# Low-rank maps and decay sums of an RWKV-7 mixer: from fp32 products to split float32r products

## The chip, the cores and the metric

The kernel runs on one core of a Trainium2 chip. The metric is the device time of one execution in microseconds (us). A core has TensorE (PE; its weight loads, PEld, run beside the products), VectorE (DVE), ScalarE (ACT), GpSimd (POOL) and SyncE (SP), whose queue issues most DMA transfers. Each engine works through its own instructions in order; semaphores make one engine wait for another.

## The reference, cut to what matters

One decoder layer over 512 tokens of width 1024: RMSNorm, one input projection that feeds two mixers (differential attention and RWKV-7 time mixing), an output projection, a layer of retrieved experts over 16384 experts, and a gated embedding. What matters here is how the time mixing gets its decay and its gate `a`:

```
w = -softplus(-(w0 + tanh(xw) @ w_up)) - 0.5      # 64 -> 512
a = sigmoid(a0 + xa @ a_up)                       # 64 -> 512
decay = exp(-exp(w))
state = state * decay + sa kk*a + v k             # token after token
```

Since exp(w) = exp(-0.5) * sigmoid(w0 + tanh(xw) @ w_up), the log of a product of decays is -exp(-0.5) times a sum of sigmoids. The kernel works in chunks of 32 tokens and needs, for each token, the sum over its chunk up to it (inclusive and exclusive) and from it to the chunk's end.

## The kernel before, in words

The 512 tokens are four blocks b of 128 (a token to a partition). The mixer stage (`mixers`) first projects the time mixing's keys, low-rank inputs, receptances and values, then walks the four blocks with `rw_prepare`, and after that solves a triangular system (`rw_solve`), builds the states (`rw_states`), and forms the outputs (`rw_out`), with the attention (`da_block`) among them. `out_proj`, the expert stage (`retrieve`, `peer`) and the tail follow.

Most products of the kernel are made from split operands: `split` has ScalarE copy x into a float32r tile hi (L129) and VectorE or GpSimd subtract, lo = x - hi (L133, L135), and three products hi·hi, hi·lo, lo·hi add up in PSUM (L201 to L203 for the input projections). The products of `rw_prepare` are plain fp32.

For a block, `rw_prepare` transposes the low-rank inputs (ptl, L466 to L468), copies two of them to SBUF (lw, L471, with a row of ones from a memset, L470, for the bias), and makes plw = lw0 · w_up (L475) and pla = lw1 · a_up (L479), each 65 rows deep and 512 columns wide. ScalarE turns them into sw and aa by a sigmoid (L477, L481). pcum = tri_le · sw (L484) and prem = tri_gt · sw (L491) are the sums over the chunk; the matrices hold -exp(-0.5) where they are not zero. ppc (L495) gives the sums of whole chunks. VectorE adds exp(-0.5) sw to pcum (e_ex, L486), and ScalarE takes the exponentials e_in, e_inv, e_ex, e_end and pcc (L487 to L497). A run of VectorE products then makes al, rt, be, kt, bh and kh, TensorE transposes four of them (ptr, L531) and makes the masked products psA (L549). Before that `rw_keys` norms the keys kk on VectorE, with a chain of 128x8 operations (L90 to L99).

The source weaves the attention's projections among the blocks as filler for TensorE (`WEAVE`: one step of eight k-chunks per yield), and in blocks 2 and 3 steps of the first solve (`PACE`). The order on each engine is laid down when the program is built, by a scheduler that starts from the source's order, takes the instructions that its estimates call ready, and gives out pages and buffers as it goes; so an instruction may stand earlier on its engine than in the source, and a tile may have to wait for the last reader of the page it got.

Memory: `p2` gives pages of 128x512 fp32 from a pool of 28, `p4` pages of 128x1024 from a pool of 14; nearly all tiles of the mixer are such pages. `small` tiles have two buffers each. PSUM accumulators `acc` have four. Constants (`mixer_consts`) are made on GpSimd at the start of the kernel; w_up and a_up, 65x512 each with the bias as last row, are loaded by four DMAs on SP's queue.

Of the kernel before, what the change touches and what calls it, by code (L numbers as in the profile page):

```python
# [8 lines left out]
F32 = mybir.dt.float32  # L9
F32R = mybir.dt.float32r  # L10
# [3 lines left out]
AF = mybir.ActivationFunctionType  # L14
OP = mybir.AluOpType
# [13 lines left out]
EXPH = math.exp(-0.5)  # L29
# [25 lines left out]
class Kernel:  # L55
# [188 lines left out]
    def mixer_consts(self, pool):  # L244
        nc, a = self.nc, self.a
# [17 lines left out]

        self.tri_le = pool.tile([128, 128], F32, name="tri_le")
        nc.gpsimd.memset(self.tri_le, -EXPH)
        same_chunk(self.tri_le, 0)
        self.tri_gt = pool.tile([128, 128], F32, name="tri_gt")
        nc.gpsimd.memset(self.tri_gt, -EXPH)
        same_chunk(self.tri_gt, 2)
        self.mask2 = pool.tile([128, 2, 128], F32, name="mask2")  # L270
# [9 lines left out]

        causal = pool.tile([128, 128], F32, name="causal")
        nc.gpsimd.memset(causal, 0.0)
# [6 lines left out]

        self.w_up = pool.tile([65, 512], F32, name="w_up")  # L290
        nc.sync.dma_start(self.w_up[0:64, :], a["rw_w_up"])
        nc.sync.dma_start(self.w_up[64:65, :], a["rw_w0"])
        self.a_up = pool.tile([65, 512], F32, name="a_up")
        nc.sync.dma_start(self.a_up[0:64, :], a["rw_a_up"])
        nc.sync.dma_start(self.a_up[64:65, :], a["rw_a0"])
        self.k_k = self.load_bcast(pool, "rw_k_k", 512)
# [106 lines left out]
    def p2(self, name, shape=(128, 512), dt=F32):  # L403
        return self.pages.tile(list(shape), dt, name=name, tag="p2", bufs=28)

# [50 lines left out]
    def rw_prepare(self, b, psum, r, k, v, kk, lx, st):  # L456

        nc = self.nc
        ident, sm, p2, p4 = self.ident, self.small, self.p2, self.p4
# [5 lines left out]
        pt = psum.tile([128, 3, 128], F32, name="ptl", tag="tp")  # L465
        nc.tensor.transpose(pt[0:64, 0, :], lx[:, 0:64], ident)  # L466
        nc.tensor.transpose(pt[0:64, 1, :], lx[:, 64:128], ident)
        nc.tensor.transpose(pt[:, 2, :], lx[:, 128:256], ident)  # L468
        lw = sm.tile([65, 2, 128], F32, name="lw")
        nc.vector.memset(lw[64:65, :, :], 1.0)  # L470
        nc.vector.tensor_copy(lw[0:64, :, :], pt[0:64, 0:2, :])  # L471
        st["lg"] = sm.tile([128, 128], F32, name="lg", bufs=NB)
        nc.vector.tensor_copy(st["lg"], pt[:, 2, :])
        p1 = psum.tile([128, 512], F32, name="plw", tag="mm")
        nc.tensor.matmul(p1, lw[:, 0, :], self.w_up, start=True, stop=True)  # L475
        sw = p2("sw")
        nc.scalar.activation(sw, p1, AF.Sigmoid)  # L477
        pa = psum.tile([128, 512], F32, name="pla", tag="mm")
        nc.tensor.matmul(pa, lw[:, 1, :], self.a_up, start=True, stop=True)  # L479
        aa = p2("aa")  # L480
        nc.scalar.activation(aa, pa, AF.Sigmoid)  # L481

        pc = psum.tile([128, 512], F32, name="pcum", tag="mm")
        nc.tensor.matmul(pc, self.tri_le, sw, start=True, stop=True)  # L484
        e_in, e_inv, e_ex, e_end = p2("e_in"), p2("e_inv"), p2("e_ex"), p2("e_end")
        nc.vector.scalar_tensor_tensor(e_ex, sw, EXPH, pc, op0=OP.mult, op1=OP.add)  # L486
        nc.scalar.activation(e_in, pc, AF.Exp)  # L487
        nc.scalar.activation(e_inv, pc, AF.Exp, scale=-1.0)
        nc.scalar.activation(e_ex, e_ex, AF.Exp)
        pr = psum.tile([128, 512], F32, name="prem", tag="mm")  # L490
        nc.tensor.matmul(pr, self.tri_gt, sw, start=True, stop=True)  # L491
        nc.scalar.activation(e_end, pr, AF.Exp)
        pp = psum.tile([128, 4, 4], F32, name="ppc", tag="tp")
# [34 lines left out]
        for src, dst in ((be, bet), (al, art[:, :, 0, :]), (rt, art[:, :, 1, :]), (kt, ktt)):  # L528
            pt = psum.tile([128, 4, 128], F32, name="ptr", tag="tp")
# [1080 lines left out]
```

## Time and profile before

| | |
|---|---|
| median of 3 runs | 1838.44 us (1831.96 to 1841.31) |
| the profiled execution | 1837.09 us, span 1835.4 us |
| granted TensorE clock, mean | 0.969 of 2.4 GHz |
| busy | PE 94%, PEld 80%, DVE 78%, ACT 41%, POOL 33% of the span |
| the four blocks of `rw_prepare` | from 104 us (first lw) to about 274 us (last akv) |

The profile is one execution; a time in it is counted from the start of its span. Busy shares are means over stages with different limits. "Granted clock" is the share of TensorE's full clock that it got; it has two levels, 0.5 (1.2 GHz) and 1.0 (2.4 GHz), and a mean between them is a mix in time.

### The profile page before, as it was taken

What the parts mean: (1) busy time and instruction counts of PE and PEld (TensorE: products, weight loads), DVE (VectorE), ACT (ScalarE), POOL (GpSimd) and SP (SyncE); (2) the same over time, 40 slices, a digit from 0 to 9 for tenths busy, and PEclk for the clock granted to TensorE, in tenths of its full rate; (3) what the DMA queues carried; (4) which work ended last, traced back from release to release, by engine and by line L of the source; (5) the groups of instructions that cost most, each with busy time, mean ns of one, the idle gap of its engine ahead of it and who ended that gap; (6) DMA issues with size and microseconds to landing.
All of it is one profiled execution on the core that took longest, in us unless ns stands there. A gap on an engine that the chain in (4) does not pass through costs nothing.

```text
span 1835.4 us, 28662 instructions
## 1 busy us (share of the span) xinstructions
PE 1728.9 (94%) x10458; PEld 1468.2 (80%) x10458; DVE 1425.6 (78%) x3216; ACT 746.7 (41%) x1382; POOL 604.7 (33%) x425
## 2 busy tenths in 40 slices
PE   7889996998899888999999999999999999999998
PEld 6766764766777787998777888889899999999986
DVE  5366787675569998888888888887888888888885
ACT  5353332432345654444344333333333333333354
POOL 2650011111046663001111133234545555555530
PEclk9896996999999999999999999999999999999999
DMA  7451233433332343446666587778989898989891
GB/s 232 137 149 55 75 114 79 129 80 127 117 120 71 125 127 115 132 139 216 206 209 197 187 272 249 254 246 292 313 302 317 300 316 303 312 303 316 303 332 58
DMA packets 150417, 363.71 MB, mean 198 GB/s; under 512 B 43922, under 2 KB 58510, under 8 KB 150148
## 3 DMA queue, kind: packets, MB, share of 16 engines
q1 hardware_dynamic: 113412, 227.65, 38.7%
q0 software_dynamic: 36864, 134.23, 21.5%
q8 instruction: 82, 1.34, 0.3%
q14 instruction: 59, 0.48, 0.1%
HBM read 332.61 MB, written 21.36 MB: 193 GB/s over the span
## 4 chain that ended last, share of the span: by engine, by line
PE 67%; DVE 19%; issue 3%; ACT 3%; POOL 0%; DMA 0%; SPq 0%; DVEq 0%; ACTq 0%; POOLq 0%
PE po L1278 21%; PE phid L1142 8%; PE phid L1144 8%; PE phid L1143 8%; PE pg L1247 2%; DVE wlo L133 2%; PE psA L549 2%; DVE ids L1091 2%; ACT whi L129 1%; DVE rest L985 1%; PE psS L765 1%; DVE jj L1235 1%; PE accr L239 1%; PE accr L237 1%; PE accr L238 1%
## 5 line engine op out<-in xcount | busy, mean ns | idle before, releaser
L133 DVE TENSOR_TENSOR wlo<-wraw,whi 128x1024 fp32r<-128x1024 f32 x243 | 297.5, 1224 | 150.6 <-ACT whi L129 150.5
L129 ACT ACTIVATE whi<-wraw 128x1024 fp32r<-128x1024 f32 x276 | 291.4, 1057 | 171.3 <-PE phid L1143 59.0
L1144 PE MATMUL phid<-u2dhi,wlo 128*128 128x384 f32 x1024 | 347.3, 339 | 12.8 <-POOL wlo L133 12.8
L1142 PE MATMUL phid<-u2dhi,whi 128*128 128x384 f32 x1024 | 350.4, 342 | 1.0 <-ACT row L1151 1.0
L1143 PE MATMUL phid<-u2dlo,whi 128*128 128x384 f32 x1024 | 346.4, 338 | 0.0
L1301 POOL DMA_INDIRECT row<-in_peer_u_dram,idx x128 | 189.8, 1483 | 403.2 <-DVE row L1313 219.7
L1301 POOL DMA_INDIRECT row<-in_peer_v_dram,idx x128 | 186.1, 1454 | 277.0 <-DVE h L1317 194.7
L1278 PE MATMUL po<-whi,chi 128*128 128x512 f32 x768 | 243.9, 398 | 1.2 <-ACT row L1151 1.2
L1278 PE MATMUL po<-whi,clo 128*128 128x512 f32 x768 | 243.1, 398 | 1.7 <-DVE clo L135 0.4
L1278 PE MATMUL po<-wlo,chi 128*128 128x512 f32 x768 | 241.4, 395 | 0.0
L1144 PEld LDWEIGHTS phid<-u2dhi,wlo 128*128 128x128 f32 x1024 | 194.3, 190 | 14.8 <-POOL wlo L133 14.7
L1142 PEld LDWEIGHTS phid<-u2dhi,whi 128*128 128x128 f32 x1024 | 194.6, 190 | 5.8 <-ACT row L1151 1.3
L1143 PEld LDWEIGHTS phid<-u2dlo,whi 128*128 128x128 f32 x1024 | 194.1, 190 | 3.7
L1278 PEld LDWEIGHTS po<-whi,clo 128*128 128x128 f32 x768 | 143.0, 188 | 42.3 <-DVE clo L135 9.0
L1278 PEld LDWEIGHTS po<-wlo,chi 128*128 128x128 f32 x768 | 144.4, 188 | 34.2
L1317 DVE SCALAR_TENSOR_TENSOR h<-row,ids,h 128x1024 f32<-128x1024 f32 x128 | 164.0, 1281 | 1.6
L129 ACT ACTIVATE chi<-gelu 128x384 fp32r<-128x384 f32 x128 | 67.4, 526 | 240.1 <-DVE gelu L1255 121.8
L1278 PEld LDWEIGHTS po<-whi,chi 128*128 128x128 f32 x768 | 141.1, 188 | 25.6 <-ACT row L1151 1.5
L1313 DVE SCALAR_TENSOR_TENSOR row<-row,xn 128x1024 f32<-128x1024 f32 x128 | 153.7, 1220 | 0.0
L1151 ACT ACTIVATE gelu<-phid 128x384 f32<-128x384 f32 x86 | 42.3, 492 | 266.9 <-PE phid L1144 266.9
L133 POOL TENSOR_TENSOR wlo<-wraw,whi 128x1024 fp32r<-128x1024 f32 x33 | 78.4, 2386 | 126.4 <-ACT whi L129 114.7
L201 PE MATMUL acc<-whi,uhi 128*128 128x512 f32 (+1 forms) x224 | 89.6, 404 | 16.7 <-ACT whi L129 9.5
(439 smaller groups left out, 2884.7 us busy)
## 6 DMA issues: line engine op xcount, KB each, us to landing
wraw<-in_peer_uT_dram SPq DMA_DIRECT2D x128, 512.0 KB
wraw<-in_peer_v_dram SPq DMA_DIRECT2D x128, 512.0 KB
wraw<-in_w_in_dram SPq DMA_DIRECT2D x24, 512.0 KB
wraw<-in_peer_w_q_dram SPq DMA_DIRECT2D x16, 512.0 KB
ahead<-row SPq DMA_DIRECT2D x42, 192.0 KB
gelu<-ahead SPq DMA_DIRECT2D x42, 192.0 KB
wraw<-in_w_out_dram SPq DMA_DIRECT2D x8, 512.0 KB
zp<-z SPq DMA_DIRECT2D x12, 224.0 KB
```

What stands on the lines that cost most here:

```text
L129: self.last_hi = nc.scalar.activation(hi, src, AF.Copy, **({} if g is None else {"scale": g}))
L133: self.last_lo = eng.tensor_tensor(lo, src, hi.bitcast(F32), op=OP.subtract)
L201: nc.tensor.matmul(o, hi[:, k, s], whi, start=(k == 0), stop=False)
L549: nc.tensor.matmul(ps[:, mm, :, :], lhs[q, m * 128:(m + 1) * 128], art[q, m, :, :], start=True, stop=True)
L1142: nc.tensor.matmul(ps, whi[:, s], hi[:, k, :], start=(k == 0), stop=False)
L1143: nc.tensor.matmul(ps, whi[:, s], lo[:, k, :], start=False, stop=False)
L1144: nc.tensor.matmul(ps, wlo[:, s], hi[:, k, :], start=False, stop=(k == KC - 1))
L1151: nc.scalar.activation(g, ps, AF.Gelu)
L1278: nc.tensor.matmul(outs[b, e], lhs[:, s], rhs[:, 512 * e:512 * e + 512], start=(c == 0 and rhs is vhi and lhs is chi), stop=(c == NKEY - 1 ...
L1301: nc.gpsimd.indirect_dma_start(out=row, out_offset=None, in_=a["peer_u" if kind == "U" else "peer_v"], in_offset=bass.IndirectOffsetOnAxis ...
L1313: nc.vector.scalar_tensor_tensor(row, row, 1.0, xn0, op0=OP.mult, op1=OP.mult, accum_out=hid0[:, k:k + 1])
L1317: nc.vector.scalar_tensor_tensor(acc0, row, hid0[:, k:k + 1], acc0, op0=OP.mult, op1=OP.add)
```

## The change

The four fp32 products per block become float32r products of split operands. w_up and a_up are split once, on GpSimd, into hi and lo; lw is split per block (hi by VectorE's copy, lo by a VectorE subtraction; row of ones: 1 in hi, 0 in lo), and plw and pla take three products each. sw is split by the helper `split` (hi by ScalarE, lo by VectorE); the triangular matrices hold 1 in place of -exp(-0.5), which float32r holds exactly, so pcum and prem take two products each. The factor -exp(-0.5) goes into the scale of the exponentials, and e_ex becomes pcum - sw. ppc is left as it is. lw's two tiles have one buffer each, where lw had two. `p2` has 26 pages where it had 28; masks are drawn up in p2 pages, and raw weights are loaded into them.

```diff
-        self.tri_le = pool.tile([128, 128], F32, name="tri_le")
-        nc.gpsimd.memset(self.tri_le, -EXPH)
-        same_chunk(self.tri_le, 0)
-        self.tri_gt = pool.tile([128, 128], F32, name="tri_gt")
-        nc.gpsimd.memset(self.tri_gt, -EXPH)
-        same_chunk(self.tri_gt, 2)
+        tri = []
+        for i in (0, 2):
+            x = self.p2("tri", [128, 128])
+            nc.gpsimd.memset(x, 1.0)
+            same_chunk(x, i)
+            tri.append(pool.tile([128, 128], F32R, name=f"tri{i}"))
+            nc.gpsimd.tensor_copy(tri[-1], x)
+        self.tri_le, self.tri_gt = tri
...
-        causal = pool.tile([128, 128], F32, name="causal")
+        causal = self.p2("causal", [128, 128])
...
-        self.w_up = pool.tile([65, 512], F32, name="w_up")
-        nc.sync.dma_start(self.w_up[0:64, :], a["rw_w_up"])
-        nc.sync.dma_start(self.w_up[64:65, :], a["rw_w0"])
-        self.a_up = pool.tile([65, 512], F32, name="a_up")
-        nc.sync.dma_start(self.a_up[0:64, :], a["rw_a_up"])
-        nc.sync.dma_start(self.a_up[64:65, :], a["rw_a0"])
+        self.w_up, self.a_up = [], []
+        for x, up, bias in ((self.w_up, "rw_w_up", "rw_w0"), (self.a_up, "rw_a_up", "rw_a0")):
+            raw = self.p2("up")
+            nc.sync.dma_start(raw[0:64, :], a[up])
+            nc.sync.dma_start(raw[64:65, :], a[bias])
+            x += [pool.tile([65, 512], F32R, name=f"{up}{y}") for y in ("hi", "lo")]
+            nc.gpsimd.tensor_copy(x[0], raw[0:65, :])
+            nc.gpsimd.tensor_tensor(x[1], raw[0:65, :], x[0].bitcast(F32), op=OP.subtract)
...
-        return self.pages.tile(list(shape), dt, name=name, tag="p2", bufs=28)
+        return self.pages.tile(list(shape), dt, name=name, tag="p2", bufs=26)
...
-        lw = sm.tile([65, 2, 128], F32, name="lw")
-        nc.vector.memset(lw[64:65, :, :], 1.0)
-        nc.vector.tensor_copy(lw[0:64, :, :], pt[0:64, 0:2, :])
+        lw = [sm.tile([65, 2, 128], F32R, name=f"lw{x}", bufs=1) for x in ("hi", "lo")]
+        for x, one in zip(lw, (1.0, 0.0)):
+            nc.vector.memset(x[64:65, :, :].bitcast(F32), one)
+        nc.vector.tensor_copy(lw[0][0:64, :, :], pt[0:64, 0:2, :])
+        nc.vector.tensor_tensor(lw[1][0:64, :, :], pt[0:64, 0:2, :], lw[0][0:64, :, :].bitcast(F32), op=OP.subtract)
...
-        p1 = psum.tile([128, 512], F32, name="plw", tag="mm")
-        nc.tensor.matmul(p1, lw[:, 0, :], self.w_up, start=True, stop=True)
+        def up(i, w, name):
+            ps = psum.tile([128, 512], F32, name=name, tag="mm")
+            nc.tensor.matmul(ps, lw[0][:, i, :], w[0], start=True, stop=False)
+            nc.tensor.matmul(ps, lw[0][:, i, :], w[1], start=False, stop=False)
+            nc.tensor.matmul(ps, lw[1][:, i, :], w[0], start=False, stop=True)
+            return ps
+        p1 = up(0, self.w_up, "plw")
         sw = p2("sw")
         nc.scalar.activation(sw, p1, AF.Sigmoid)
-        pa = psum.tile([128, 512], F32, name="pla", tag="mm")
-        nc.tensor.matmul(pa, lw[:, 1, :], self.a_up, start=True, stop=True)
+        swh, swl = (p2(x, dt=F32R) for x in ("swhi", "swlo"))
+        self.split(swh, swl, sw)
+        pa = up(1, self.a_up, "pla")
         aa = p2("aa")
         nc.scalar.activation(aa, pa, AF.Sigmoid)
         pc = psum.tile([128, 512], F32, name="pcum", tag="mm")
-        nc.tensor.matmul(pc, self.tri_le, sw, start=True, stop=True)
+        for x, y in ((swh, True), (swl, False)):
+            nc.tensor.matmul(pc, self.tri_le, x, start=y, stop=not y)
...
-        nc.vector.scalar_tensor_tensor(e_ex, sw, EXPH, pc, op0=OP.mult, op1=OP.add)
-        nc.scalar.activation(e_in, pc, AF.Exp)
-        nc.scalar.activation(e_inv, pc, AF.Exp, scale=-1.0)
-        nc.scalar.activation(e_ex, e_ex, AF.Exp)
+        nc.vector.tensor_tensor(e_ex, pc, sw, op=OP.subtract)
+        nc.scalar.activation(e_in, pc, AF.Exp, scale=-EXPH)
+        nc.scalar.activation(e_inv, pc, AF.Exp, scale=EXPH)
+        nc.scalar.activation(e_ex, e_ex, AF.Exp, scale=-EXPH)
         pr = psum.tile([128, 512], F32, name="prem", tag="mm")
-        nc.tensor.matmul(pr, self.tri_gt, sw, start=True, stop=True)
-        nc.scalar.activation(e_end, pr, AF.Exp)
+        for x, y in ((swh, True), (swl, False)):
+            nc.tensor.matmul(pr, self.tri_gt, x, start=y, stop=not y)
+        nc.scalar.activation(e_end, pr, AF.Exp, scale=-EXPH)
```

## Rows read from the trace of the kernel before

**Rows 1.** The page: busy time by engine, and the last chain by line.

```profile
PE 1728.9 (94%) x10458; PEld 1468.2 (80%) x10458; DVE 1425.6 (78%) x3216; ACT 746.7 (41%) x1382; POOL 604.7 (33%) x425
...
PE po L1278 21%; PE phid L1142 8%; PE phid L1144 8%; PE phid L1143 8%; PE pg L1247 2%; DVE wlo L133 2%; PE psA L549 2%; DVE ids L1091 2%; ACT whi L129 1%; DVE rest L985 1%; PE psS L765 1%; DVE jj L1235 1%; PE accr L239 1%; PE accr L237 1%; PE accr L238 1%
```

**Rows 2.** Windows: length, busy us (and instructions) by engine, granted clock, DMA.

```profile
128.00:170.00 42.00, 32.13 (x113) 22.02 (x112) 27.41 (x69) 16.52 (x28) 2.28 (x2) 0.63 0.25 78
...
196.00:262.00 66.00, 62.07 (x288) 44.62 (x288) 60.15 (x175) 31.65 (x55) 2.04 (x5) 0.95 0.27 79
```

**Rows 3.** Chain of waits in order of time (start, us, what), block 2.

```profile
199.65 0.23 PE acc L201
199.88 0.86 PE pcum L484 x2
```

**Rows 4.** The same chain after block 1 and in block 3.

```profile
172.57 0.43 PE acc L202
...
241.68 1.71 PE pcum L484 x2
```

**Rows 5.** Groups by line: ScalarE's split copy (min/median/max ns), VectorE's subtraction and copy (mean).

```profile
L129 ACT ACTIVATE u2hi<-tps x8: 577/597/598, 488.5 to 496.3; 128x512 fp32r<-128x512 f32 x8
...
L133 DVE TENSOR_TENSOR u2lo<-tps,u2hi 128x512 fp32r<-128x512 f32 x8 | 5.4, 690 | 2.1 <-ACT u2hi L129 2.0
...
L471 DVE COPY lw<-ptl 64x256 f32<-64x256 f32 x4 | 1.6, 410 | 6.0 <-PE ptl L468 6.0
```

**Rows 6.** Timeline of all engines in block 0; in brackets the idle time before.

```profile
127.91 1.12 DVE L90 TENSOR_SCALAR knxh<-knr 128x8 f32<-128x8 f32 x1
...
129.08 1.27 POOL L437 TENSOR_TENSOR zs<-z,zp 128x512 f32<-128x512 f32 x1
...
130.42 0.17 DVE L97 TENSOR_TENSOR knxi<-knx,knxh 128x8 f32<-128x8 f32 x1
...
133.04 0.68 DVE L486 SCALAR_TENSOR_TENSOR e_ex<-sw,pcum 128x512 f32<-128x512 f32 x1
...
138.14 0.69 DVE L510 TENSOR_TENSOR be<-aa,e_inv 128x512 f32<-128x512 f32 x1
...
138.98 1.08 PE L531 MATMUL ptr<-ident,be 128*128 128x128 f32 x4 [7.09 <-DVE be L510]
```

**Rows 7.** Chain of waits in order of time, block 1.

```profile
162.67 1.72 PE pla L479 x2
...
164.49 0.27 DVE lw L470
...
167.03 0.61 DVE e_ex L486
...
169.82 0.59 ACT z L879
```

**Rows 8.** Timeline of all engines in block 2.

```profile
207.30 0.68 DVE L510 TENSOR_TENSOR be<-aa,e_inv 128x512 f32<-128x512 f32 x1
...
210.26 0.60 PE L531 MATMUL ptr<-ident,be 128*128 128x128 f32 x4
```

**Rows 9.** Waits from 225 to 262 us: who waited for whom, total, times, longest.

```profile
DVE e_ex L486 <- PE pcum L484: 0.9, 1, 0.9
```

**Rows 10.** Tile zp: GpSimd's first operation on it after the set-up.

```profile
L434 POOL TENSOR_TENSOR zp<-zp,z x16: 743/1286/1748, 38.8 to 126.1; 128x512 f32<-128x512 f32 x12, 128x256 f32<-128x256 f32 x4
```

**Rows 11.** Windows as in rows 2, around block 0's end and in block 1.

```profile
134.00:136.00 2.00, 0.00 (x0) 0.00 (x0) 2.00 (x4) 1.89 (x4) 0.00 (x0) 0.60 0.32 103
...
144.00:146.00 2.00, 1.30 (x6) 0.47 (x5) 1.19 (x4) 0.00 (x0) 0.00 (x0) 0.84 0.27 87
...
148.00:150.00 2.00, 2.00 (x8) 1.48 (x7) 0.74 (x3) 0.00 (x0) 0.00 (x0) 0.52 0.37 78
```

**Rows 12.** Waits from 270 to 480 us, as in rows 9.

```profile
POOL bv L692 <- DMA pd<-pp: 15.4, 1, 15.4
...
ACT pexp L770 <- issue: 12.3, 1, 12.3
```

## The prediction

> **What bounds the kernel now.** I read the page first. TensorE is busy for most of the span, and most of the chain that ended last lies on it [rows 1]; but the lines that carry that chain are those of the expert stage (L1142 to L1144, L1278), and the change touches none of them. It touches the mixer: sixteen products (four in each of four token blocks of rw_prepare), their preparation, and the pool of pages they live in. So its worth is read from the stretch of those four blocks, 104 to 262 us, and the page's shares say nothing of it. The windows show two regimes there [rows 2]. From 128 to 170 us TensorE is busy 32.13 of 42 us at a mean granted clock of 0.63: nothing fills its gaps, and what counts is the latency through ScalarE and VectorE. From 196 to 262 us TensorE (62.07 of 66) and VectorE (60.15 of 66) are both nearly full. Only in the second regime can saved TensorE time become saved time, and there added VectorE time costs nearly as much. What the mixer saves or loses passes on to the end: out_proj and the expert stage begin when it is done.
>
> **The change, priced.** A fp32 product of 512 columns runs as two instructions and takes 0.86 us at 2.4 GHz, a float32r product 0.23 [rows 3]. At 1.2 GHz they take 1.71 and 0.43 us [rows 4]. A block loses four fp32 products and gains ten float32r ones (3+3+2+2): 3.44 - 2.33 = 1.11 us saved at the high level, 6.84 - 4.3 = 2.54 at the low one. Blocks 0 and 2 are at the high level, 1 and 3 mostly at the low one: 7.3 us of TensorE time in all.
>
> Added per block: one ScalarE copy of 128x512 into fp32r (the nearest row, from PSUM: 0.597 us), one VectorE subtraction of 128x512 (nearest row 690 ns; back to back such operations start 0.60 apart), a subtraction of 64x256 (the copy of that shape takes 0.41) [rows 5] and one more memset (0.27) [rows 7]. The e_ex operation keeps its engine, shape and class; the factor inside the exponentials is a scale that e_inv has already: both nothing. ScalarE is idle around each addition, except that aa now starts one copy (0.5 to 0.6 us) after sw; aa is not needed before ka, so I cost that at nothing; without that cover it is 0.6 a block.
>
> What matters is the new wait. Before, pcum needed sw alone. Now its second half needs sw, then the ScalarE copy, then a VectorE subtraction that queues in order behind the thirteen small operations of the key norm (L90 to L99, L451). Behind the waiting pcum stand prem, ppc and all later TensorE work; e_ex and the exponentials wait for it. Block by block:
>
> Block 0. TensorE stands idle 7.09 us until be is there (138.14) [rows 6], so its saving is worth nothing. VectorE runs without a gap from the key norm through e_ex (133.04) to be. The subtraction adds 0.6 to that run, and if it stands after kk, pcum's second half and its hand-over come between (0.4 to 0.6 more), partly filled by the two wlo operations behind e_ex. Bounds +0.6 and +1.8; I take +0.9, nearest the VectorE row.
>
> In block 0 the rows also show VectorE's 128x8 operation L90 taking 1.12 us while GpSimd works on zp and zs, where one of that size right after them takes 0.17; GpSimd's last such operation runs 129.08 to 130.35 [rows 6]. By the Trainium skill (SBUF — State Buffer, section "Who interferes with whom") a VectorE instruction with two SBUF inputs and a GpSimd instruction that reads SBUF exclude each other for the whole instruction; the new subtraction has two such inputs. The trace agrees that one can hold the other. By that rule the subtraction could start up to 1.27 us late here and the sum below would be +1.7 in place of +0.4; by the rows alone it stands in the queue behind the key norm, whose first operations are held already, and pays nothing more. I go by the row.
>
> Block 1. The chain runs pla, a memset of lw for a later block that waits for pla at the head of VectorE's queue, the key norm, e_ex, the exponentials, the eviction z, TensorE again [rows 7]. plw and pla shrink by 0.42 each (1.71 - 3 x 0.43), so the memset gets free 0.84 earlier; there are two of them now (+0.2), and the subtraction adds 0.6, perhaps with pcum's second half (0.43 and the hand-over) behind it. ScalarE's sw stays where its table load puts it. Bounds -0.3 and +0.7; I take +0.2. The rest of the saving is idle time before z.
>
> Block 2. Here TensorE is on the chain with projections as filler: -1.11 at best. Against it: lo and hi of lw have one buffer each instead of two, so the memsets for block 3 now wait for block 2's pla, about 0.8 us, at the head of VectorE's queue, and the subtraction comes after: e_ex up to 1.8 us later. That is nearly covered: be was ready at 207.98 and TensorE turned to it at 210.26 [rows 8], 2.3 us of slack. Bounds -1.1 and +0.7; I take -0.4.
>
> Block 3. At the low level from plw on [rows 4]: plw, pla and pcum shrink, less the stall for the subtraction, which queues among the solver's VectorE steps: about -1.2 on TensorE. VectorE gets 1.0 more but loses a wait of 0.9 for pcum [rows 9]. The two meet again at ptr (258 us), near level: bounds -1.2 and +1.0; I take -0.3.
>
> Set-up. GpSimd makes masks and casts them, and now splits w_up and a_up (two casts, two subtractions of 65x512; nearest row 1.27 for 128x512 [rows 6]). The loads are the same four on SP's queue, the results are not wanted before block 0, and the next work in GpSimd's queue, zp, begins at 38.8 us [rows 10]. So nothing; the upper bound is 2.6, were VectorE held for both subtractions while TensorE waits for it.
>
> Sum: +0.9 + 0.2 - 0.4 - 0.3 = **+0.4 us**, against the profiled execution's 1837.09 (span 1835.4, 1.7 around it). The median of the runs shown, 1838.44, lies 1.35 above that. 0.4 on it gives **1838.8**, said as 1839. With all lower bounds (-2.0) 1836.4; with all upper ones, set-up and port included (+8.1), 1846.5.
>
> **Rivals.** (A) TensorE is the bound in all four blocks and the whole 7.3 us is kept: 1831.1. For it: its share of the windows from 196 us on. Against it: the 7.09 us wait in block 0 and the chain through VectorE in block 1. Chance 0.13.
>
> (B) The clock. It falls in 134 to 136 us (mean 0.60), after TensorE had stood idle since 132, and again at 148 (0.52 in 148 to 150) after TensorE was busy only 1.30 us of 144 to 146 [rows 11]. From there to the end of pla at 164.39 TensorE works at 1.2 GHz and is nearly all of the chain: 16.4 us of it would be 8.2 at 2.4 GHz. The change puts prem and ppc later, into the hole before 138.98, and shifts every later phase by some tenths; the second fall need not come. With block 3 kept whole (2.54) this gives 1838.44 - 10.7 = 1827.7. Against it: the work that precedes the fall is untouched. The same lottery can lose in block 2, which ran at 1.00. Chance 0.17.
>
> (C) Slower: pages. The p2 pool goes from 28 pages to 26, and each block holds two more for a while (swhi, swlo). By the code, v, qT, rtT and dav hold 16 pages until the end of the mixer, and in the mixer's last part two solver pages, up to five states, y, ysq, rwg, bv, the loads bhr and ykr and the pp pages come on top: about 28. The trace shows page waits there: bv waited 15.4 us for the store of pp, and an exponential waited 12.3 us on ScalarE with no releaser shown [rows 12], which I read as a wait for a page of p4. bv's wait cost nothing. If two pages fewer put such a wait on SP's queue (bhr and ykr, with the loads of the next block behind them) or on a state, the mixer's rw chain stops for about that long: 1838.8 + 12.3 = 1851. It decides as soon as the waiting page is not bv's. Against it: by my count the four blocks themselves need about 25. Chance 0.18.
>
> **The numbers.** Forecast 0.52, A 0.13, B 0.17, C 0.18. A measurement of this kernel can tell about 0.5%, 9.2 us, from no change: faster means under 1829.2, slower over 1847.6. B and the best of A (0.03) are faster: 0.20. C is slower: 0.18. The rest is the same: 0.62. The forecast's own range is 1836 to 1847; taking in A, most of B and C leaves 1826 to 1851, with under 2 in 10 outside.
>
> **What would show it.** Right: pcum's second product in each block waits for the subtraction, TensorE's wait for be in block 0 is no shorter, be comes 0.5 to 2 us later there, memsets of lw hold VectorE in blocks 1 and 2, and the mixer ends within 3 us of before. Wrong: 196 to 262 us gets shorter by over 3 us (A); the clock is 1.00 in 148 to 164 (B); states, SP loads or evictions after 282 us wait with no work of their own outstanding (C).

## The result, and the profile after

The changed kernel takes **1853.34 us** (median of 18 runs, 1842.18 to 1863.07), the kernel before 1841.76 in 18 runs of the same session: a ratio of **1.0066, interval 1.0044 to 1.0087**, some 12 us slower. The forecast was 1839, no change, and the median lies above the range's end of 1851. The profiled execution has a span of 1847.2 us and a mean granted clock of 0.961 (before 1835.4 and 0.969).

The page of the changed kernel: busy time by engine and the last chain by line, as [rows 1].

```profile
PE 1738.3 (94%) x10466; PEld 1475.7 (80%) x10466; DVE 1429.3 (77%) x3228; ACT 759.8 (41%) x1394; POOL 609.1 (33%) x431
...
PE po L1295 21%; PE phid L1159 8%; PE phid L1161 8%; PE phid L1160 8%; PE pg L1264 2%; DVE wlo L133 2%; PE acc L202 2%; ACT whi L129 2%; PE acc L203 2%; PE acc L201 2%; DVE ids L1108 1%; PE psA L566 1%; PE psS L782 1%; DVE rest L1002 1%; DVE jj L1252 1%
```

TensorE was to lose 7.3 us of work and is 9.4 us longer busy: less work, but at a lower clock. ScalarE grew by 13.1 us where four copies of 0.6 us were expected. The windows that answer to [rows 2]:

```profile
128.00:170.00 42.00, 25.15 (x113) 18.00 (x113) 31.07 (x75) 22.27 (x33) 1.15 (x1) 0.70 0.21 64
...
196.00:262.00 66.00, 59.41 (x268) 44.35 (x268) 58.09 (x170) 34.16 (x55) 0.86 (x4) 0.87 0.22 65
```

In the first stretch TensorE is busy 7.0 us less and ScalarE 5.8 us more than before; the second is 2.7 us less busy on TensorE, with 20 products fewer in it and at a clock of 0.87 in place of 0.95. ScalarE's growth is in its table loads. The groups by line, kernel after (30 loads in all):

```profile
L491 ACT ACT_TABLE_LOAD x4 | 5.1, 1283 | 0.1
L514 ACT ACT_TABLE_LOAD x4 | 5.1, 1283 | 0.1
L496 ACT ACT_TABLE_LOAD x4 | 5.1, 1283 | 0.0
L503 ACT ACT_TABLE_LOAD x4 | 5.1, 1283 | 2.6 <-issue 2.5
```

and kernel before (22 in all; these are the ones of `rw_prepare`):

```profile
L477 ACT ACT_TABLE_LOAD x4 | 5.1, 1283 | 0.1
...
L487 ACT ACT_TABLE_LOAD x3 | 3.8, 1283 | 0.1
...
L497 ACT ACT_TABLE_LOAD x1 | 1.3, 1283 | 0.0
```

Two loads a block became four: 8 x 1.283 = 10.3 us of ScalarE. Block 0 shows why. ScalarE's timeline, kernel before:

```profile
128.47 0.60 ACT L477 ACTIVATE sw<-plw 128x512 f32<-128x512 f32 x1
128.97 0.59 ACT L481 ACTIVATE aa<-pla 128x512 f32<-128x512 f32 x1
...
130.79 1.28 ACT L497 ACT_TABLE_LOAD   x1
132.09 0.18 ACT L497 ACTIVATE pcc<-ppc 128x16 f32<-128x16 f32 x1
133.80 0.60 ACT L487 ACTIVATE e_in<-pcum 128x512 f32<-128x512 f32 x1 [1.53 <-issue]
```

and after:

```profile
125.56 0.60 ACT L491 ACTIVATE sw<-plw 128x512 f32<-128x512 f32 x1
...
126.66 0.62 ACT L129 ACTIVATE swhi<-sw 128x512 fp32r<-128x512 f32 x1
127.30 1.28 ACT L514 ACT_TABLE_LOAD   x1
128.59 0.18 ACT L514 ACTIVATE pcc<-ppc 128x16 f32<-128x16 f32 x1
128.79 1.28 ACT L496 ACT_TABLE_LOAD   x1
130.09 0.60 ACT L496 ACTIVATE aa<-pla 128x512 f32<-128x512 f32 x1
133.24 1.28 ACT L503 ACT_TABLE_LOAD   x1 [2.55 <-issue]
134.53 0.60 ACT L503 ACTIVATE e_in<-pcum 128x512 f32<-128x512 f32 x1
```

The copy of sw took aa's place behind sw, and ppc, which still needs sw alone, now runs on TensorE ahead of pcum. So the scheduler let pcc's small exponential in between the two sigmoids. ScalarE changes from the sigmoid's table to the exponential's, back for aa, and once more for e_in, the last time on the way to be. From the start of sw to the first ptr (the transposes that end a block's preparation) it was 10.5, 16.3, 12.3 and 18.0 us in the four blocks; it is 14.1, 20.1, 13.0 and 18.5.

By the Trainium skill (ScalarE: Activation LUTs, section "Table sets: the hidden batching unit") a kernel does all calls of one table before it changes to another. This order breaks that rule, and each change of table shows as a load of 1.28 us in the trace. The Trainium skill (ScalarE: Activation LUTs, section "What ACT_TABLE_LOAD costs") counts a drain of about 1.38 us beside each load of 1.283; here, where ScalarE has work ready, it starts 0.01 to 0.05 us after the load, and no drain shows.

The other thing is the new wait. Waits of TensorE's products on tile pcum (who kept the engine idle: us in all, times), kernel before, after, and with the subtraction on GpSimd (e12 below):

```profile
  ACT sw L477: 0.7, 1
```
```profile
  DVE swlo L133: 4.2, 2
```
```profile
  POOL swlo L133: 1.4, 1
```

TensorE stands 4.2 us for swlo, with everything that is queued behind pcum: 3.3 us in block 0 and 0.9 in block 1. In blocks 2 and 3 other products fill the time, and in block 3 it is VectorE that waits. Block 3's timeline, kernel after (rows of these tiles):

```profile
240.92 0.63 ACT L129 ACTIVATE swhi<-sw 128x512 fp32r<-128x512 f32 x1
...
243.78 0.70 DVE L133 TENSOR_TENSOR swlo<-sw,swhi 128x512 fp32r<-128x512 f32 x1
...
245.31 0.63 PE L500 MATMUL pcum<-swhi,tri 128*128 128x512 f32 x1
...
248.30 0.63 PE L500 MATMUL pcum<-swlo,tri 128*128 128x512 f32 x1
248.97 0.69 DVE L502 TENSOR_TENSOR e_ex<-pcum,sw 128x512 f32<-128x512 f32 x1 [3.52 <-PE pcum L500]
```

swlo waits 2.2 us in VectorE's queue and is done at 244.48. The second half of pcum still comes only 3 us after the first, since the scheduler put six projection products between the two, and VectorE waits 3.52 us for it where it waited 0.9 [rows 9].

**Where the rest went.** The four blocks end nearly where they did (last akv 275.0 against 274.2), which hid all this: that execution reached the first plw at 101.0 in place of 105.1, because its clock did not fall in 45 to 60 us, and the fall of 148 to 164 us [rows 11] did not come either. The loss in sight lies later, in stages with no changed instruction. Windows of the kernel after, and of before with the same stage:

```profile
374.00:382.00 8.00, 6.50 (x95) 5.07 (x96) 7.42 (x25) 3.87 (x10) 0.00 (x0) 1.00 0.27 58
382.00:392.00 10.00, 10.00 (x34) 4.92 (x35) 4.67 (x12) 3.25 (x9) 3.22 (x3) 0.53 0.41 106
```
```profile
376.00:384.00 8.00, 6.70 (x107) 5.70 (x107) 6.97 (x25) 5.03 (x14) 0.00 (x0) 1.00 0.22 44
384.00:394.00 10.00, 9.94 (x96) 6.08 (x95) 6.09 (x11) 1.87 (x4) 3.22 (x3) 1.00 0.68 156
```

After nearly the same stretch (busy 6.50 and 6.70 of 8 us) the clock falls to 1.2 GHz in one execution, until 403 us, and stays up in the other. Summed over windows of 5 us, TensorE's busy time times (1 less the clock) is 42.3 us before and 54.2 after: 11.9 more, beside 11.8 of span. That sent the first experiments after the clock and the pages.

### The profile page after: what moved, and what is told of

It is laid out like the page before. It is cut to its first block, busy times and chain, and to the rows that moved or that the text cites. A ratio compares the mean times of both kernels' runs of the same rounds, so it can differ in the third digit from the quotient of the medians.

```text
span 1847.2 us, 28710 instructions
## 1 busy us (share of the span) xinstructions
PE 1738.3 (94%) x10466; PEld 1475.7 (80%) x10466; DVE 1429.3 (77%) x3228; ACT 759.8 (41%) x1394; POOL 609.1 (33%) x431
## 4 chain that ended last, share of the span: by engine, by line
PE 69%; DVE 21%; issue 4%; ACT 4%; DMA 1%; POOL 1%; SPq 0%; DVEq 0%; ACTq 0%; POOLq 0%
PE po L1295 21%; PE phid L1159 8%; PE phid L1161 8%; PE phid L1160 8%; PE pg L1264 2%; DVE wlo L133 2%; PE acc L202 2%; ACT whi L129 2%; PE acc L203 2%; PE acc L201 2%; DVE ids L1108 1%; PE psA L566 1%; PE psS L782 1%; DVE rest L1002 1%; DVE jj L1252 1%
## 5 line engine op out<-in xcount | busy, mean ns | idle before, releaser
L1168 ACT ACTIVATE gelu<-phid 128x384 f32<-128x384 f32 x86 | 42.3, 492 | 266.9 <-PE phid L1161 223.5
```

Of the source, the lines that this page charges most:

```text
L1168: nc.scalar.activation(g, ps, AF.Gelu)
```

## The experiments

Each result carries the mean granted clock of its timed runs. Over 310 timed executions, a line with one slope and a height for each kernel gives 13.9 us for 0.01 of clock, with a scatter of 2.1 us; the 125 of the kernel before alone give 13.4, correlation -0.93. The last column is an estimate: each kernel's mean time moved along that line to a clock of 0.967. It takes the clock out also where the edit is what lowered it, and it supposes that a difference of clock between two kernels costs what one between two executions of a kernel does.

| kernel | median us | ratio to before, interval | mean clock | at 0.967 |
|---|---|---|---|---|
| before (125 runs) | 1838.9 | | 0.968 | 1840.3 |
| after | 1853.3 | 1.0066 [1.0044, 1.0087] | 0.959 | 1842.3 |
| e1 26 pages | 1840.3 | 1.0004 [0.9978, 1.0030] | 0.968 | 1841.5 |
| e2 maps only | 1841.0 | 1.0002 [0.9973, 1.0031] | 0.965 | 1837.9 |
| e3 sums only | 1858.1 | 1.0103 [1.0058, 1.0148] | 0.959 | 1846.9 |
| e4 filled waits | 1869.0 | 1.0163 [1.0119, 1.0207] | 0.955 | 1852.6 |
| e5 after, delay 2 | 1855.7 | 1.0096 [1.0066, 1.0126] | 0.959 | 1842.9 |
| e6 after, delay 4 | 1853.9 | 1.0077 [1.0049, 1.0106] | 0.959 | 1842.6 |
| e7 before, delay 2 | 1837.9 | 0.9994 [0.9973, 1.0016] | 0.968 | 1840.4 |
| e8 before, delay 4 | 1837.0 | 0.9987 [0.9961, 1.0012] | 0.969 | 1839.9 |
| e9 before, 30 loads | 1848.0 | 1.0048 [1.0018, 1.0078] | 0.965 | 1845.4 |
| e10 aa first | 1859.5 | 1.0104 [1.0074, 1.0135] | 0.955 | 1842.3 |
| e11 pcc behind aa | 1853.9 | 1.0055 [1.0021, 1.0089] | 0.959 | 1841.7 |
| e12 swlo on GpSimd | 1845.2 | 1.0039 [0.9995, 1.0083] | 0.963 | 1840.3 |
| k1 single product | 1835.2 | 0.9987 [0.9967, 1.0006] | 0.967 | 1834.6 |
| k2 padded | 1847.9 | 1.0045 [1.0019, 1.0070] | 0.964 | 1842.6 |
| k3 other order | 1847.0 | 1.0050 [1.0033, 1.0066] | 0.962 | 1839.3 |
| k4 filled hole | 1846.6 | 1.0039 [1.0012, 1.0067] | 0.960 | 1836.8 |
| n1 after, old order | 1851.6 | 1.0068 [1.0043, 1.0092] | 0.961 | 1842.5 |
| n2 maps + single | 1844.3 | 1.0043 [1.0019, 1.0068] | 0.959 | 1834.8 |

**Pages, and the two halves of the change.** e1 is the kernel before with the smaller pool:

```
-        return self.pages.tile(list(shape), dt, name=name, tag="p2", bufs=28)
+        return self.pages.tile(list(shape), dt, name=name, tag="p2", bufs=26)
```

> The kernel before with 26 pages in place of 28 and nothing else; all its instructions stand in the same order. Theory P (pages: some load, state or eviction waits for a page, and the 12 us are that wait): 8 to 12 us slower than before. Theory K (clock: the four changed blocks end 0.8 us later and the rest is TensorE at its low level in stretches that hold no changed instruction, 382 to 402 us above all): pages play no part, within 4 us of before, and y of the last block ends within 2 us of 427.4.

Two pages fewer cost nothing: rival C falls. e2 keeps the diff's `up` products and 26 pages and leaves pcum, prem, the masks and the exponentials as before; e3 is the other half, with 28 pages.

> Only the low-rank maps (plw, pla) split; sums of decays in fp32 as before; 26 pages. Theory P: 8 to 12 us slower than before, since it has 26 pages too. Theory K: the time follows the clock. Summed over 5 us windows, TensorE's busy time times (1 less the granted clock) is 42.3 us before and 54.2 after, 11.9 more, beside 11.8 us of span; so this kernel's span less that sum is within 3 us of 1793 (before 1793.1, after 1793.0). Theory W (the work of the split of sw and its wait is what costs): within 3 us of before.

> Only the sums of decays (pcum, prem) split, with the factor moved; low-rank maps in fp32 as before; 28 pages. Theory P: within 4 us of before. Theory W: the whole 10 to 12 us. Theory K: span less the clock's sum within 3 us of 1793 again, wherever the span comes out.

The maps cost nothing that can be told; the sums carry the whole loss and more, and e3 has the 30 table loads where e2 has 22. Span less the clock's sum came to 1789 for e2 and 1798 for e3, outside the 3 us both times and on opposite sides. No more can be read from it: two kernels with the products of before give 1785 (k3) and 1797 (e7).

**Filling the short waits** (36 products whose results are overwritten, held behind the last instruction ahead of the wait):

```
+    def warm(self, ps, n, first, cols=512):
+        for _ in range(n):
+            self.behind(self.nc.tensor.matmul(ps[:, :cols], self.tri_le[0:65, :], self.w_up[0][:, :cols],
+                                              start=True, stop=True, skip_group_check=True), first)
...
+        self.warm(po.rearrange("p h v -> p (h v)"), 3, last)
```

> The changed kernel with 36 products whose results are overwritten, put into the short waits of TensorE ahead of the stretch at the low level (ahead of po, of the first pmt and of prp, in every block). Theory K: the clock stays at 2.4 GHz from 380 to 402 us or nearly so, and the time comes down by 4 to 10 us from the changed kernel's 1853, less up to 3 us for the products themselves. Theory P and W: the same as the changed kernel or up to 8 us slower (36 products of 0.1 to 0.23 us at the high level).

A miss: 16 us slower than the changed kernel, and the clock was at 0.50 from 375 to 390 us all the same. TensorE had been busy without a gap ahead of it:

```profile
366.00:374.00 8.00, 8.00 (x61) 5.17 (x57) 6.12 (x20) 1.94 (x5) 2.82 (x3) 1.00 0.47 152
374.00:384.00 10.00, 10.00 (x47) 5.03 (x46) 5.01 (x19) 3.33 (x10) 0.00 (x0) 0.50 0.44 115
```

The short waits are not what lets it fall there. Why the fill costs 16 us was not found; at equal clock 10 are left.

**A pure delay.** Two or four copies of a solver page onto itself at the end of the second solve; every other instruction keeps its place in its queue.

```
+        if half:
+            for _ in range(2):
+                nc.vector.tensor_copy(xf, xf)
```

> The changed kernel with two copies of a solver page onto itself put at the end of the second solve, a pure delay of about 1.3 us at 312 us; every engine's other instructions stand in the same order. Theory F (fixed: the same instructions that stand ahead of the stretch at the low level bring the fall wherever they run): the fall comes at the same instruction, the first pmt and prp of block 2, about 1.3 us later, and the time is 1.3 us over the changed kernel's, 1854 to 1856. Theory L (where the stretch happens to lie in time decides whether the clock falls in it): the stretches at the low level after 312 us are others, and the median moves by more than 4 us either way from 1853, not by the delay; at equal mean clock (14.4 us for each 0.01, from 77 runs) it is 1.3 us over the changed kernel.

> The same with four copies, a delay of about 2.7 us. Theory F: fall at the same instruction, time 1855 to 1858. Theory L: other stretches at the low level than with two copies, median more than 4 us from 1856 for at least one of the two; at equal mean clock 2.7 us over the changed kernel.

> The kernel before with the same two copies at the same place. Theory F: no fall between 375 and 405 us, as before; time 1.3 us over before, 1840 to 1843. Theory L: a fall can come where there was none, and then the time is 8 to 12 us over before; with no fall it is 1.3 us over.

> The kernel before with four copies. Theory F: no fall between 375 and 407 us, 1841 to 1845. Theory L: as with two copies, a fall in this one, in that one, in both or in neither; in at least one of the four kernels with a delay the state of the clock in that stretch is the opposite of what it is without the delay.

Windows of e5 (the changed kernel delayed, same stage as above) and of e8 (the kernel before delayed):

```profile
376.00:384.00 8.00, 6.63 (x95) 5.07 (x93) 7.42 (x24) 3.68 (x10) 0.00 (x0) 1.00 0.27 59
384.00:394.00 10.00, 9.87 (x67) 5.82 (x68) 6.27 (x14) 3.45 (x10) 3.22 (x3) 1.00 0.56 121
```
```profile
372.00:380.00 8.00, 7.81 (x57) 4.22 (x57) 4.66 (x12) 3.85 (x12) 1.95 (x2) 0.57 0.37 84
380.00:390.00 10.00, 10.00 (x31) 6.01 (x30) 2.07 (x4) 0.60 (x1) 1.26 (x1) 0.50 0.40 106
```

The fall is gone from the changed kernel and has come to the kernel before, so it belongs to neither: theory F falls. But the medians did not move by more than 2.3 us, so L, which wanted 4, falls with it. The one fall that the profile put forward comes and goes between executions. The execution of e5 that shows none took 1841.47 us, the fastest of its five; e6's shows none either and took 1851.41, and the medians of both stay 14 us or more above before.

These profiles show where the time goes. Up to 312 us the kernels before, e1, e7 and e8 have the same order of the same instructions; from the first plw to the last akv they take 169.1, 170.4, 164.8 and 162.6 us, mean 166.7. After, e4, e5, e6 and n1 share the changed blocks: 174.0, 174.1, 174.7, 179.4 and 174.1, mean **175.3**. So the four blocks cost 8.6 us; the profile of before happened to be one of the long ones, and only the comparison of single executions had made them look equal. The whole stretch of the blocks in the kernel before and after:

```profile
105.10:274.20 169.10, 153.86 (x699) 113.03 (x698) 124.09 (x330) 69.67 (x114) 24.18 (x23) 0.88 0.32 92
```
```profile
101.00:275.00 174.00, 147.91 (x702) 111.68 (x701) 131.26 (x343) 82.64 (x126) 22.18 (x19) 0.87 0.29 83
```

TensorE is idle for 15.2 us of it before and 26.1 after. Over the four and the five profiles the means are 16.2 and 25.4: 9.2 us more idle time. Its busy time is nearly the same, 150.5 and 149.8, for the shorter products meet more time at 1.2 GHz (32.4 and 49.8 us). What follows the blocks takes 1565.0 and 1566.2 us, e4 with its added products left aside: the changed kernels spend more of it at 1.2 GHz (79.6 us against 70.2) and have less idle time on TensorE (68.2 against 75.2). So in these profiles the loss lies in the blocks, and in TensorE's waits there.

**The order that adds the table loads.** e9 forces the changed order of ScalarE on the kernel before:

```
-        nc.scalar.activation(aa, pa, AF.Sigmoid)
+        aa_act = nc.scalar.activation(aa, pa, AF.Sigmoid)
...
-        nc.scalar.activation(st["pc"], pp, AF.Exp)
+        self.behind(aa_act, nc.scalar.activation(st["pc"], pp, AF.Exp))
```

> The kernel before with one order added: aa's sigmoid stands behind the small exponential pcc on ScalarE, as it came to stand in the changed kernel. That makes 30 table loads in place of 22 (8 more of 1.28 us) and changes nothing else of the work; products in fp32, 28 pages. Theory T (table loads: what costs the 12 us is that ScalarE swaps its table twice more in each block, on the way to the exponentials, and the rest follows from it): 7 to 13 us slower than before, 1846 to 1853, with e_in later in every block. Theory W (the added copy, subtraction and wait of the split itself): within 3 us of before. Theory K (the shorter float32r products leave TensorE less busy and the clock falls more often): within 3 us of before, mean clock 0.967 as before.

ScalarE in block 0 of e9:

```profile
132.25 1.28 ACT L497 ACT_TABLE_LOAD   x1
133.96 0.18 ACT L497 ACTIVATE pcc<-ppc 128x16 f32<-128x16 f32 x1 [0.42 <-PE ppc L495]
134.16 1.28 ACT L481 ACT_TABLE_LOAD   x1
135.45 0.60 ACT L481 ACTIVATE aa<-pla 128x512 f32<-128x512 f32 x1
137.20 1.28 ACT L487 ACT_TABLE_LOAD   x1 [1.15 <-issue]
138.49 0.60 ACT L487 ACTIVATE e_in<-pcum 128x512 f32<-128x512 f32 x1
```

Slower by 0.18 to 0.78% (8.8 us in the middle), with blocks of 176.6 us in which TensorE is idle for 22.7: so far theory T holds. The scheduler also placed some other work anew, so the loads are not quite the only difference. Taking the loads out of the changed kernel, by the program's order (e10: the split's two lines moved behind aa's sigmoid) or by one dependency (e11: the line above the other way round, pcc behind aa):

> The changed kernel with pla's product and aa's sigmoid ahead of the split of sw in the program: 22 table loads again, everything else of the change kept. Theory T: 8 to 13 us faster than the changed kernel, 1840 to 1845; from the first ptl to the last akv 168 to 171 us, as in the kernel before (mean 168.0 of four profiles), where the changed kernel takes 177.3 (mean of three). Theory W: at most 3 us faster than the changed kernel. Theory K: still 1850 or more, mean clock still 0.959.

> The changed kernel with one order added: pcc's exponential stands behind aa's sigmoid on ScalarE; the copy of sw keeps its place ahead of aa. 22 table loads. Theory T: as e10 within 3 us, 1840 to 1846: the copy ahead of aa costs nothing by itself. Theory W: 1850 or more.

Both have 22 loads, and both are misses: without the loads the kernel is no faster, so theory T does not hold as the whole account. In e10's profile the blocks take 184.4 us, 73 of them at 1.2 GHz, where 168 to 171 was expected. In e11 the four ways from sw to ptr shrink to 12.3, 17.4, 12.2 and 18.7 us, 5 less in sum, as they should. But in block 3 TensorE stands for arb, an operation of VectorE, as it does nowhere in block 3 of the changed kernel:

```profile
268.62 2.71 PE L566 MATMUL psA<-art,beT 64*128 64x256 f32 x8 [4.28 <-DVE arb L571]
```

Its blocks take 179.9 us with 26.4 idle, and they run into a fall that the changed kernel's do not have; the same window of e11 and of after:

```profile
272.00:282.00 10.00, 10.00 (x38) 8.04 (x37) 2.94 (x9) 0.25 (x1) 0.00 (x0) 0.50 0.34 95
```
```profile
272.00:282.00 10.00, 10.00 (x55) 7.84 (x54) 0.58 (x2) 5.65 (x8) 5.06 (x6) 1.00 0.58 169
```

and its mean clock is no higher than the changed kernel's. e12 is e10 with `self.split(swh, swl, sw, nc.gpsimd)`:

> As e10, and the subtraction that makes swlo moved from VectorE to GpSimd, out of the queue behind the key norm. If that queue still costs time once the table loads are gone, 1 to 4 us faster than e10, most of it in block 3, where pcum waited longest; if GpSimd's slower operation (1.27 us against 0.69) and its hold on VectorE cost more, up to 3 us slower.

14 us faster than e10, where 1 to 4 was expected. TensorE's wait for swlo falls to 1.4 us (3.7 in e10), the two halves of pcum stand 0.9 us apart in block 3, and the blocks take 170.1 us. Of the kernels with the whole change this one is the fastest; its interval to before just takes in no change.

**What sets the mean clock?** k1 makes the products short and adds nothing: sw is written as float32r and pcum and prem are one product each.

> The kernel before with sw written as float32r and pcum and prem as one float32r product each in place of an fp32 one; the low halves are left out, so there is no copy, no subtraction, no new wait and no table load more. TensorE has 1.26 us less to do in each block at the high level (2 x 0.63). Theory K (less for TensorE to do, so the clock falls more often): mean clock 0.960 to 0.964 and 3 to 8 us slower than before in spite of less work. Theory O (the order of the later work has its own mean clock): anything from 0.955 to 0.970. Theory W (the added operations and waits cost, through their holes): clock 0.967 and 0 to 4 us faster than before.

Theory K falls: less work on TensorE, and the clock as before. Without the split of sw the saving may show: 3.0 us between the means of the session (1835.1 against 1838.1), though the interval takes in no change.

k2 gives TensorE its time back (one product more in each `up`, two more on each of pcum and prem); k3 only changes the order in which the sources of ptr are transposed; k4 is e12 with 16 products ahead of the first ptr.

> As e12 (aa first, swlo by GpSimd) with products repeated so that plw, pla, pcum and prem take TensorE as long as in fp32: 6 float32r products more in each block (plw and pla four each, pcum and prem four each), each overwritten by the real ones. Theory K: mean clock back to 0.966 or more and 1838 to 1843. Theory O or W: clock as in e12 (0.963) or lower, 1845 to 1850, the added products costing up to 3 us.

> The kernel before with one change of order in the program: rt is transposed ahead of al. The same operations and transfers; the scheduler makes another order of the later work (33 places on TensorE, 30 on VectorE). Theory K and W: within 3 us of before, clock 0.967. Theory O: a clock of its own, 0.958 to 0.965, and 3 to 12 us slower than before.

> As e12 with 16 float32r products put into TensorE's longest wait of the mixer, ahead of the first transposes of block 0 (7 us idle), overwritten by the transposes. If the idle time there is what lets the clock fall in 134 to 180 us: no fall there, block 0 from plw to the next plw 50 us or less in place of 53.0, and 2 to 6 us faster than e12. If not: as e12 or up to 2 us slower.

k2 does not bring the clock back. k3 does the same work as before and is 0.33 to 0.66% slower at a clock of 0.962: two thirds of the clock's loss without any added work. So an order alone can cost about as much as e9's. The profiles tell the two apart: in k3's blocks TensorE is idle for 16.2 us, as before, and 54.6 of their 172.2 us are at 1.2 GHz; in e9's it is idle for 22.7, with 44.4 at 1.2 GHz. k4 is no test of the hole as meant: the scheduler put only 11 of the products into it, behind pcum's second half, where TensorE first stood 4.40 us. TensorE's timeline of k4:

```profile
135.78 0.80 PE L505 MATMUL pcum<-swlo,tri 128*128 128x512 f32 x1 [4.40 <-POOL swlo L133]
...
136.80 4.89 PE L448 MATMUL ptr<-rw_w_uphi,tri 65*128 65x512 f32 x11
```

They also held the real ptr back to 141.5.

n1 gives the changed kernel the order of before for all work behind the blocks, by dependencies of order alone between neighbours in the recorded queues; n2 joins e2 and k1 with that order.

> The changed kernel, all its operations kept, 30 table loads too; order-only dependencies give each engine's work behind the four blocks (from the second solve to the retrieval) the order that it has in the kernel before. Theory O (the order of the later work sets the mean clock): mean clock 0.964 to 0.968 and 1842 to 1847, so 6 to 11 us faster than the changed kernel, what is left over before being the blocks. Theory B (what the blocks do to the clock and to the time is all): 1850 to 1856, clock 0.958 to 0.960.

> The low-rank maps split as in the changed kernel, the sums of decays as one float32r product each of sw written as float32r (low halves left out; no copy, subtraction or wait), 22 table loads, the later work in the order of before. From the two parts alone (e2 at equal clock 2.2 us faster than before, k1 5.6): with a clock of 0.967, 1831 to 1836; if the order does not carry the clock, 1836 to 1846.

n1 tests less than was meant: behind the blocks the two orders turned out to differ in one transposition on TensorE and some six operations on VectorE, so n1 is the changed kernel once more, and its time says so (1.0068). That excludes the later order as the cause here. n2 is with k1 the best of all at equal clock, and its clock is 0.959: no version is faster than the kernel before beyond its interval.

## Why the prediction was wrong

**The step that failed first** is "aa now starts one copy (0.5 to 0.6 us) after sw; aa is not needed before ka, so I cost that at nothing", with "ScalarE's sw stays where its table load puts it". I priced the late aa by who needs aa, and not by what the scheduler would put in its place. pcc went there, and with it two table loads a block, one on the way to the exponentials. e9 shows what that order costs the kernel before: 8.8 us. The cover that I named for aa was real; the order was not. It is not shown that the loads are the whole loss of the changed kernel: e10 and e11 have none of them and are no faster.

**Block 0**, "+0.9, nearest the VectorE row": 10.5 us from sw to ptr became 14.1, so +3.6, twice the upper bound. e11 without the loads has 12.3: 1.8 goes with the split and its wait, at the bound, and 1.8 with the loads. **Block 1**, "+0.2": +3.8, of which 2.7 goes with the loads. **Blocks 2 and 3** had gains in the forecast and got +0.7 and +0.5; the stall of pcum in block 3 was named, but not that VectorE would wait 3.52 us there. The sum of +0.4 stands against 8.6 measured over executions, with 9.2 us more idle time on TensorE in the blocks. These ways from sw to ptr are of one profile each, and the clock is in them.

**The saving** of 7.3 us was counted as mostly lost. At equal clock k1 and e2 gain 5.7 and 2.4 us, which would make it about right in size and nearly all kept. In the same account the loads cost 5.1 (e9 less before), the changed kernel stands at +2.0, and so some 5 us are left for the copy, the subtraction and the wait. That is a sum of estimates that rest on the line of the clock, not a measurement.

**The baseline.** I summed against one execution and took its fall at 148 us as the kernel's own. With the same instructions in the same order e8 had none there and took 6.5 us less for its blocks. That "the mixer ends within 3 us of before" came true and proved nothing.

**The clock.** Rival B foresaw one fall that would not come; in the profile after it did not come, and the kernel is slower all the same. The sum held no cost of clock. By the line, 0.968 to 0.959 at 13.9 us for 0.01 would be about 12 of the 14 us between the means (1853.5 and 1839.2). The profiles do not bear that out as a cost of its own: of their 8.5 us between the spans, e4 aside, nearly all lies in the blocks, where TensorE waits more, and behind them more time at 1.2 GHz is made up by less idle time. The profiled executions of the changed blocks ran at a mean clock of 0.963, above the 0.959 of all their runs, so what the slower executions lose beside the blocks left no profile. How much of the loss is the clock's is open. **Rival A** fails, **rival C** is refuted by e1, and the durations of the added operations (0.62, 0.69) are what was said; the set-up and the factor in the exponentials show no cost.

The weighed rule on VectorE and GpSimd (SBUF — State Buffer, section "Who interferes with whom", of the Trainium skill) agrees again: three 128x8 operations ahead of swlo in block 0, two of them with two inputs in SBUF, took 1.12 to 1.18 us beside GpSimd in place of 0.17. swlo itself took 0.69 and was not held, as I chose; but two of the held ones end between the end of swhi (127.28) and its own start (130.84), so the hold reached it through the queue.

**Open** is what sets the mean clock. Shown not to: the pages (e1), shorter products alone (k1), a shift of the later work by 1 to 3 us (e5 to e8), its order (n1), the table loads alone (e9 lost only 0.002 to 0.003, e11 won nothing back). A change of order can do it (k3, where it differs inside the blocks and behind them). In all five profiles with the changed blocks it also falls once between 490 and 535 us, in work that the change does not touch, and of the four with the old blocks only in e1's; why was not found.

## What to carry to other kernels

When an operation is slipped in behind an activation, write down the whole order of that engine with its tables: a copy costs 0.6 us, an exponential that slips between two sigmoids costs two loads of 1.28. A split of an intermediate on the critical path puts a copy and a queued subtraction between two products; splitting the maps' constants and lw (e2) cost nothing that could be told. And where executions differ by 20 us through the clock, one profile is no baseline: compare medians first, and stage lengths over several profiles.

## What the runs showed of the hardware

The mean granted clock goes with most of the spread between executions of one kernel (1826 to 1853 us for the kernel before, correlation -0.93). Two kernels of the same work can differ in it lastingly: 0.968 before, 0.962 in k3. Whether it falls in a given stage differs between executions of the same instructions: around 150 us it falls in the profiles of before and e1 and not in those of e7 and e8, whose only edit lies behind 300 us. It can also fall right after a stretch without a wait: in e4 TensorE was busy for 8.00 of the 8 us ahead of it. A table load took 1.283 us in each of the 30, and ScalarE's next work, where it was ready, began 0.01 to 0.05 us after.
